# The value product of the forgetting-attention heads in float32r: value parts side by side, softmax weights split at PSUM eviction

## The chip, the cores and the metric

The kernel runs on one core of a Trainium2 chip. The metric is the device time of one execution in microseconds (us), the median of several runs. A core has TensorE for matrix products (PE; PEld is its weight load), VectorE (DVE), ScalarE (ACT) and GpSimd (POOL) for elementwise work, and SyncE (SP), which here issues the DMA transfers. TensorE reads its operands from the on-chip memory SBUF and writes to PSUM; GpSimd doesn't read PSUM in this kernel. The engines run on their own and wait for each other by semaphores.

## The reference

Two layers of a decoder trunk, 256 tokens of width 1024, all in float32. A layer is a half-step SwiGLU feed-forward part, a mixer and a second feed-forward part. The mixer projects the normalized input once (`W_in`), splits the result into three groups of attention heads (A: 4 heads, B: 4, C: 8, head width 64) and projects their outputs back (`W_out`). The change concerns group C, forgetting attention:

```python
def forgetting_attention(q, k, v, log_f):
    c = jnp.cumsum(log_f, axis=1).transpose(0, 2, 1)
    def block(i):
        ...
        s = jnp.einsum('bqhd,bkhd->bhqk', qb, k).astype(jnp.float32) * scale
        s = s + cq[..., None] - c[:, :, None, :]
        s = jnp.where((key_pos[None, :] <= qpos[:, None])[None, None], s, -jnp.inf)
        p = jax.nn.softmax(s, axis=-1).astype(v.dtype)
        return jnp.einsum('bhqk,bkhd->bqhd', p, v)
    ...
# in the mixer:
    o_c = forgetting_attention(cq, ck, cv.reshape(B, S, C_HEADS, HEAD_DIM), log_f)
    o_c = o_c * jax.nn.sigmoid(cg)
    return jnp.concatenate([o_a, o_b, o_c], axis=-1) @ w_out
```

## The kernel before

**Numbers.** The large products are done in float32r, a float32 format with a shortened mantissa. A float32 operand x is written as a high part (x converted to float32r) and a low part (x minus the high part, converted as well), and a product is the sum of three: high by high, high by low, low by high (`mm3`, L295). Weights arrive as `raw` tiles; ScalarE makes the high part `wh` (L117), VectorE the low part `wl` (L121), some units ahead of their use (`pump`). Scores, transposes and value products of the heads are plain float32 matmuls. `mm(o, l, r)` (L292) computes l transposed times r: l is loaded as weights, r streams through, and every matmul of this kind has L293 in the profile.

**Order.** The order of the instructions on each engine is written out by hand, one queue per engine, each worked off in order. In the mixer the eight projection chunks `iq, ib, b, a, ck, cq, cv, cg` follow one another; each takes two PSUM banks of the tag `gu` (4 banks in rotation) and 4 steps, and a `post_` function then moves the result out. `post_cv` (L819) moves the values of the C heads with ScalarE into `va`, whose slots 5 to 12 are the C heads' (slot 0 is A's, 1 to 4 are B's), each 64 columns and a column of ones, with which the value product also gives the sum of the softmax weights. The A and B heads run as side work between steps of the projection, on PSUM banks of the tag `acc`.

**The C heads** run after the projection, from L966, on the banks of `gu`, with the output projection of A's and B's results between them as filler: `out_halves` yields after every 12 matmuls into the `acc` banks, and after every second half it splits one more unit of weights (`W.pump`). In turn i of the loop (L970 to L985) come:

- `scores(i)`: two matmuls into a bank; VectorE adds the mask and takes the maximum (L848);
- `flip(i-1)`: TensorE transposes the three 128x128 blocks of the softmax weights p (L862), and one copy takes them to SBUF as `pT` (L864): on ScalarE for odd heads, on VectorE for even ones;
- `exps(i)`: two exponentials on ScalarE (L855, L856);
- the next 12 matmuls of the output projection;
- `values(i-1)`: three matmuls, pT's blocks as weights against 65 columns of `va`; VectorE takes the reciprocal of the sums (L878) and, for each half of the tokens, multiplies by it and by the gate `sg` on the way out of PSUM (L884);
- from time to time `outT` (transposes of a finished pair of heads, L895, and its split into high and low, L902 and L903) and `c_T` (the transposes of later heads' queries and keys, L962, L963).

After the loop, `tail` finishes the output projection.

Of the kernel before, what the change touches and what calls it, by code (L numbers as in the profile page):

```python
# [10 lines left out]
F32 = mybir.dt.float32  # L11
F32R = mybir.dt.float32r
I32 = mybir.dt.int32
AF = mybir.ActivationFunctionType
ALU = mybir.AluOpType
# [3 lines left out]
P = 128  # L19
# [122 lines left out]
def kernel(ctx: ExitStack, tc: tile.TileContext, x, ffn1_norm, ffn1_w_gate, ffn1_w_up, ffn1_w_down,  # L142
# [3 lines left out]
    cp = ctx.enter_context(tc.tile_pool(name="cp", bufs=1))  # L146
# [6 lines left out]
    at = ctx.enter_context(tc.tile_pool(name="at", bufs=1))  # L153
    pp = ctx.enter_context(tc.tile_pool(name="pp", bufs=2))
# [3 lines left out]
    V, A, G, T = nc.vector, nc.scalar, nc.gpsimd, nc.tensor  # L158

    def bank(tag):  # L160
        return psum.tile([P, 512], F32, name="ps_" + tag, tag=tag)

    def tmp(n):
        return tp.tile([P, 512], F32, name="tmp", tag="tmp")[:, :n]
# [14 lines left out]

    ones = cp.tile([P, P], F32, name="ones")  # L180
    G.memset(ones, 1.0)
    minus_half = cp.tile([P, 32], F32, name="minus_half")
    G.memset(minus_half, -0.5)
    nc.scalar.dma_start(cst[:, 0:P], const[:, 0:P])
# [96 lines left out]
    causal = cp.tile([P, 3 * P], F32, name="causal")  # L281
    cqa = [at.tile([P, 8, 66], F32, name=f"cqa{t}", tag=f"cqa{t}") for t in range(2)]
    cka = [at.tile([P, 8, 66], F32, name=f"cka{t}", tag=f"cka{t}") for t in range(2)]
    va = [at.tile([P, 13, 65], F32, name=f"va{t}", tag=f"va{t}") for t in range(2)]
    for t in range(2):
        G.memset(cqa[t][:, :, 65:66], 1.0)
        G.memset(cka[t][:, :, 64:65], 1.0)
        G.memset(va[t][:, :, 64:65], 1.0)

    hres = xp.tile([P, KT, S], F32, name="hres")  # L290

    def mm(o, l, r, start, stop):  # L292
        T.matmul(o, l, r, start=start, stop=stop, skip_group_check=True)  # L293
# [253 lines left out]
    def mixer(l, norm, nxt):  # L547
# [12 lines left out]
        def heads(ap, n):  # L560
            return ap.rearrange("p (h d) -> p h d", h=n)
# [28 lines left out]
        def evac(dst, ps, t, scale=None):  # L590
            A.activation(dst, ps, AF.Copy, scale=norm.r[:, t:t + 1])
# [226 lines left out]

        def post_cv(ps):  # L819
            for t in range(2):  # L820
                evac(va[t][:, 5:13, 0:64], heads(ps[t], 8), t)

        def post_cg(ps):
            hr = sm.tile([P, 2], F32, name="hr", tag="hr")
# [9 lines left out]
        def run_heads(hs, qk, tag, emit=None, lag=1):  # L834
            pj, pt, op = {}, {}, {}

            def scores(i):

                kind, h = hs[i]
                q, k = qk(h)  # L840
                b = bank(tag)
                mm(b[:, 0:P], q[:, 0:P], k[:, 0:P], True, True)
                mm(b[:, P:3 * P], q[:, P:S], k[:, 0:S], False, True)
                mask = st["amask"] if kind == "A" else causal
                s = tmp(3 * P)
                nm = sm.tile([P, 2], F32, name="nm", tag="nm")
                for t, c in enumerate((slice(0, P), slice(P, 3 * P))):
                    V.tensor_tensor_reduce(s[:, c], b[:, c], mask[:, c], -1.0, 3e38, op0=ALU.add, op1=ALU.min,  # L848
                                           accum_out=nm[:, t:t + 1])
                pj[i] = (s, nm)  # L850

            def exps(i):
                s, nm = pj[i]
                p = pp.tile([P, 3 * P], F32, name="p", tag="p", bufs=2)
                A.activation(p[:, 0:P], s[:, 0:P], AF.Exp, bias=nm[:, 0:1], scale=-1.0)  # L855
                A.activation(p[:, P:3 * P], s[:, P:3 * P], AF.Exp, bias=nm[:, 1:2], scale=-1.0)  # L856
                pj[i] = p

            def flip(i):
                b = bank(tag)  # L860
                for j in range(3):
                    T.transpose(b[:, j * P:(j + 1) * P], pj[i][:, j * P:(j + 1) * P], ident)  # L862
                d = pp.tile([P, 3 * P], F32, name="pT", tag="pT")
                (A.copy if i % 2 == (emit is None) else V.tensor_copy)(d, b[:, :3 * P])  # L864
                pt[i] = d
                del pj[i]

            def values(i):
                kind, h = hs[i]
                vi = dict(A=0, B=1 + h, C=5 + h)[kind]  # L870
                e = i % 2
                b = bank(tag)[:, :130].rearrange("p (t c) -> p t c", t=2)
                d = pt.pop(i)
                mm(b[:, 0], d[:, 0:P], va[0][:, vi], True, True)
                mm(b[:, 1], d[:, P:2 * P], va[0][:, vi], False, False)
                mm(b[:, 1], d[:, 2 * P:3 * P], va[1][:, vi], False, True)
                ri = sm.tile([P, 2], F32, name="ri", tag="ri")
                V.reciprocal(ri, b[:, :, 64])  # L878
                if e == 0:
                    op[i // 2] = pp.tile([P, 2, P], F32, name="o", tag="o")  # L880
                o = op[i // 2][:, :, e * HD:(e + 1) * HD]
                if kind == "C":
                    for t in range(2):
                        V.scalar_tensor_tensor(o[:, t], b[:, t, 0:64], ri[:, t:t + 1],  # L884
                                               st["sg"][:, t, h * HD:(h + 1) * HD], op0=ALU.mult, op1=ALU.mult)
                else:
                    V.tensor_tensor(o, b[:, :, 0:64], ri[:, :, None].to_broadcast([P, 2, HD]), op=ALU.mult)

            def outT(i):
                kind, h = hs[2 * i]  # L890
                k = dict(A=0, B=2, C=4)[kind] + h // 2
                o = op.pop(i)
                b = bank(tag)
                for t in range(2):
                    T.transpose(b[:, t * P:(t + 1) * P], o[:, t], ident)  # L895
                if k < 6:
                    hh = hp.tile([P, S], F32R, name="oh", tag="hh")
                    hl = hp.tile([P, S], F32R, name="ol", tag="hl")
                else:
                    both = tp.tile([P, 512], F32R, name="ohl", tag="tmp")  # L900
                    hh, hl = both[:, :S], both[:, S:]
                A.copy(hh, b[:, :S])  # L902
                V.tensor_tensor(hl, b[:, :S], hh.bitcast(F32), op=ALU.subtract)  # L903
                oT[k] = (hh, hl)

            if emit is None:
                return scores, exps, flip, values, outT
            for i, (kind, h) in enumerate(hs):
                emit(i, lambda i=i: (scores(i), exps(i)))
                emit(i + lag, lambda i=i: flip(i))  # L910
                emit(i + lag + 1, lambda i=i: values(i))
                if i % 2:
                    emit(i + lag + 3, lambda i=i: outT(i // 2))

        oT = {}
        posts = dict(iq=post_iq, ib=post_ib, a=post_a, b=post_b, ck=post_ck, cq=post_cq, cv=post_cv, cg=post_cg)
        for name, cols in CHUNKS:
            n = sum(c[1] for c in cols)
            ps = [bank("gu") for _ in range(2)]
# [71 lines left out]
    def before_mixer(l):  # L991
        if l == 0:
            turn_gains(1)
            turn_gains(2)
            V.memset(causal[:, P:2 * P], 0.0)
            for t in range(2):
                V.tensor_scalar(causal[:, 2 * t * P:(2 * t + 1) * P], future, NEG, None, op0=ALU.mult)
        mixer_tables(l)
# [4 lines left out]
    norm = Norm(0, 0)  # L1003
# [35 lines left out]
    for mp in range(4):  # L1039
        ks = range(2 * mp, 2 * mp + 2)  # L1040
# [30 lines left out]
    for l in range(DEPTH):  # L1071
        norm = ffn(norm, lambda: Norm(1, l), lambda: before_mixer(l), g0 if l == 0 else None)
        norm = mixer(l, norm, lambda: Norm(2, l))
        norm = ffn(norm, (lambda: Norm(0, l + 1)) if l + 1 < DEPTH else None)
# [35 lines left out]
```

## Time and profile before

| | |
|---|---|
| median of 3 runs | 1068.8 us (1068.74 to 1068.98) |
| the profiled execution | 1069.04 us, of which the profile's span is 1067.3 us |
| PE busy | 1059.1 us |
| DVE, ACT busy | 820.6 us, 583.6 us |

How to read it: the profile is of one execution. Busy time is the time in which an engine has an instruction under way; TensorE's matmuls overlap, so the length of one record is not what it costs in a row of them, and the step from one start to the next is. The granted clock is 1.00 at full speed. In a row of a group, the last column before the bar is the count, then come the busy time in us, the mean length in ns, and the idle time of the engine just before.

### The profile page before, as it was taken

What the parts mean: (1) busy time and instruction counts of PE and PEld (TensorE: products, weight loads), DVE (VectorE), ACT (ScalarE), POOL (GpSimd) and SP (SyncE); (2) the same over time, 40 slices, a digit from 0 to 9 for tenths busy, and PEclk for the clock granted to TensorE, in tenths of its full rate; (3) what the DMA queues carried; (4) which work ended last, traced back from release to release, by engine and by line L of the source; (5) the groups of instructions that cost most, each with busy time, mean ns of one, the idle gap of its engine ahead of it and who ended that gap; (6) DMA issues with size and microseconds to landing.
All of it is one profiled execution on the core that took longest, in us unless ns stands there. A gap on an engine that the chain in (4) does not pass through costs nothing.

```text
span 1067.3 us, 16804 instructions
## 1 busy us (share of the span) xinstructions
PE 1059.1 (99%) x6571; PEld 944.9 (89%) x6571; DVE 820.6 (77%) x1547; ACT 583.6 (55%) x998; POOL 162.0 (15%) x188
## 2 busy tenths in 40 slices
PE   9999999999999999999999999999999999999998
PEld 8999999987889899999989999999877998888887
DVE  5998777779766797777779877777796668977774
ACT  5665554666554565555456555546765455655551
POOL 2004000277400100000010200003865000000000
PEclk9999999999999999999999999999999999999999
DMA  9576464464332365554645565555554313664631
GB/s 323 203 238 205 157 233 151 148 211 157 121 117 80 119 223 178 191 198 158 198 158 184 190 226 167 189 173 176 164 170 141 119 41 121 235 235 150 207 119 39
DMA packets 130911, 181.79 MB, mean 170 GB/s; under 512 B 7008, under 2 KB 104720, under 8 KB 130832
## 3 DMA queue, kind: packets, MB, share of 16 engines
q1 hardware_dynamic: 130512, 180.65, 50.1%
q8 instruction: 51, 0.84, 0.3%
q14 instruction: 28, 0.23, 0.1%
q10 hardware_dynamic: 320, 0.08, 0.0%
HBM read 179.67 MB, written 1.05 MB: 169 GB/s over the span
## 4 chain that ended last, share of the span: by engine, by line
PE 97%; DVE 1%; DMA 1%; ACT 0%; SPq 0%; issue 0%
PE ps_gu L293 64%; PE ps_acc L293 31%; PE ps_gu L962 1%; DVE xhl L320 1%; DMA xin<-in_x_dram 1%; PE ps_acc L862 0%; PE ps_gu L862 0%; PE ps_acc L598 0%; DVE hres L352 0%; ACT xhl L317 0%; PE ps_gu L895 0%; PE ps_acc L383 0%; PE ps_acc L895 0%; DVE tmp L424 0%; ACT rb L349 0%
## 5 line engine op out<-in xcount | busy, mean ns | idle before, releaser
L121 DVE TENSOR_TENSOR wl<-raw,wh 128x1024 fp32r<-128x1024 f32 (+2 forms) x343 | 418.4, 1227 | 20.6 <-ACT wh L117 20.3
L293 PE MATMUL ps_gu<-xhl,wh 128*128 128x512 f32 (+1 forms) x1408 | 352.7, 392 | 3.5 <-DVE tmp L424 2.6
L117 ACT CAST wh<-raw 128x1024 fp32r<-128x1024 f32 (+2 forms) x343 | 345.1, 1034 | 12.3 <-PE ps_gu L293 6.8
L293 PEld LDWEIGHTS ps_gu<-xhl,wh 128*128 128x128 f32 x1408 | 253.6, 189 | 51.6 <-DVE xhl L320 2.9
L293 PEld LDWEIGHTS ps_gu<-xhl,wl 128*128 128x128 f32 x1400 | 191.5, 190 | 13.5
L293 PE MATMUL ps_gu<-xhl,wl 128*128 128x256 f32 x1400 | 197.3, 283 | 0.0
L293 PE MATMUL ps_gu<-wh,xhl 128*128 128x512 f32 (+2 forms) x512 | 163.7, 385 | 0.0
L424 DVE TENSOR_TENSOR tmp<-ps_gu,tmp 128x256 f32<-128x256 f32 x175 | 74.1, 424 | 111.2 <-ACT tmp L423 110.9
L293 PE MATMUL ps_acc<-hl,wh 128*128 128x256 f32 x528 | 149.7, 284 | 0.0
L293 PE MATMUL ps_acc<-hh,wh 128*128 128x256 f32 x528 | 149.4, 283 | 0.0
L293 PE MATMUL ps_acc<-hh,wl 128*128 128x256 f32 x528 | 149.4, 283 | 0.0
L423 ACT COPY tmp<-ps_gu 128x256 f32<-128x256 f32 x175 | 64.7, 370 | 128.6 <-PE ps_gu L293 123.1
L293 PEld LDWEIGHTS ps_gu<-wh,xhl 128*128 128x128 f32 x512 | 94.8, 188 | 22.1 <-issue 7.3
L293 PEld LDWEIGHTS ps_acc<-hl,wh 128*128 128x128 f32 x528 | 101.4, 192 | 0.3
L293 PEld LDWEIGHTS ps_acc<-hh,wl 128*128 128x128 f32 x528 | 101.4, 192 | 0.0
L293 PEld LDWEIGHTS ps_acc<-hh,wh 128*128 128x128 f32 x528 | 101.4, 192 | 0.0
L293 PE MATMUL ps_gu<-wl,xhl 128*128 128x512 f32 (+2 forms) x256 | 95.8, 374 | 0.0
L331 POOL TENSOR_TENSOR ssacc<-ssacc,tmp 128x512 f32<-128x512 f32 x10 | 12.9, 1294 | 509.8 <-ACT tmp L329 329.8
L431 ACT ACTIVATE tmp<-tmp 128x256 f32<-128x256 f32 x88 | 36.8, 418 | 85.2 <-DVE tmp L429 85.2
L440 ACT CAST hh<-tmp 128x256 fp32r<-128x256 f32 x80 | 32.6, 407 | 87.9 <-DVE tmp L436 87.9
L293 PEld LDWEIGHTS ps_gu<-wl,xhl 128*128 128x128 f32 x256 | 48.3, 189 | 6.3
L429 DVE TENSOR_TENSOR tmp<-tmp,rb 128x256 f32<-128x256 f32 x88 | 37.8, 430 | 3.0
(241 smaller groups left out, 1204.2 us busy)
## 6 DMA issues: line engine op xcount, KB each, us to landing
raw<-in_ffn_w_down_dram SPq DMA_DIRECT2D x44, 1024.0 KB, 6.7
raw<-in_ffn_w_gate_dram SPq DMA_DIRECT2D x43, 1024.0 KB, 7.0
raw<-in_ffn_w_up_dram SPq DMA_DIRECT2D x43, 1024.0 KB, 5.2
raw<-in_w_in_dram SPq DMA_DIRECT2D x24, 1024.0 KB, 5.2
raw<-in_w_out_dram SPq DMA_DIRECT2D x8, 1024.0 KB, 4.9
raw<-in_w_in_dram SPq DMA_DIRECT2D x4, 768.0 KB, 4.8
raw<-in_w_in_dram SPq DMA_DIRECT2D x4, 656.0 KB, 4.4
xin<-in_x_dram SPq DMA_DIRECT2D x4, 256.0 KB, 5.2
```

The lines of the kernel that those rows point to most:

```text
L117: self.nc.scalar.copy(hv, src)
L121: (engine or self.nc.vector).tensor_tensor(lv, self.srcs[self.n_low], hv.bitcast(F32), op=ALU.subtract)
L293: T.matmul(o, l, r, start=start, stop=stop, skip_group_check=True)
L320: V.scalar_tensor_tensor(self.l[:, m], hres[:, m] if src is None else src, gT[:, self.col + m:self.col + m + 1], self.h[:, m].bitcast(F32) ...
L331: G.tensor_tensor(self.acc, self.acc, sq, op=ALU.add)
L423: A.copy(o, ps[:, 1])
L424: V.tensor_tensor(o, ps[:, 0], o, op=ALU.add)
L429: V.tensor_tensor(t_, t_, norm.rb, op=ALU.mult)
L431: A.activation(th, t_, AF.Tanh, scale=0.5)
L440: (V.tensor_copy if late else A.copy)(hh, t_)
L962: T.transpose(b[:66, i * S + t * P:i * S + (t + 1) * P], src[t][:, 2 * hp_ + i, :], ident)
```

## The change

- The values of the C heads move out of `va` (now 5 slots) into new float32r tiles `vc`, one for each half of the tokens: per head a high part and a low part side by side, each 66 columns: 64 of the value, one that is 1 in the high part and 0 in the low part, and one that is 0. The constant columns are written once at the start (a new memset `zeros` on GpSimd, two copies per tile on VectorE).
- `post_cv`: ScalarE writes the high part, VectorE the low part (PSUM times the norm factor, minus the high part).
- `flip` for C heads: ScalarE copies PSUM to the high half of `pT` (float32r), then VectorE subtracts that from the PSUM block into the low half. For A and B heads it stays as it was.
- `values` for C heads: six float32r matmuls in place of three float32 ones. For each block, the high softmax weights against both value parts (132 columns), then the low weights against the high value part (66 columns). The result has two halves per token block; ScalarE copies the second one (64 columns for each half of the tokens) to SBUF, VectorE adds the first one to it, and the two final multiplications read that sum from SBUF in place of PSUM.

```diff
+    zeros = cp.tile([P, 32], F32, name="zeros")
+    G.memset(zeros, 0.0)
...
-    va = [at.tile([P, 13, 65], F32, name=f"va{t}", tag=f"va{t}") for t in range(2)]
+    va = [at.tile([P, 5, 65], F32, name=f"va{t}", tag=f"va{t}") for t in range(2)]
+    vc = [at.tile([P, 8, 2, 66], F32R, name=f"vc{t}", tag=f"vc{t}") for t in range(2)]
...
+        V.tensor_copy(vc[t][:, :, :, 64:66], zeros[:, 0:32].rearrange("p (a b c) -> p a b c", a=8, b=2))
+        V.tensor_copy(vc[t][:, :, 0, 64], ones[:, 0:8])
...
         def post_cv(ps):
             for t in range(2):
-                evac(va[t][:, 5:13, 0:64], heads(ps[t], 8), t)
+                h, lo = vc[t][:, :, 0, 0:64], vc[t][:, :, 1, 0:64]
+                evac(h, heads(ps[t], 8), t)
+                V.scalar_tensor_tensor(lo, heads(ps[t], 8), norm.r[:, t:t + 1], h.bitcast(F32), op0=ALU.mult,
+                                       op1=ALU.subtract)
...
-                d = pp.tile([P, 3 * P], F32, name="pT", tag="pT")
-                (A.copy if i % 2 == (emit is None) else V.tensor_copy)(d, b[:, :3 * P])
+                if hs[i][0] == "C":
+                    d = pp.tile([P, 2, 3 * P], F32R, name="pTC", tag="pT")
+                    A.copy(d[:, 0], b[:, :3 * P])
+                    V.tensor_tensor(d[:, 1], b[:, :3 * P], d[:, 0].bitcast(F32), op=ALU.subtract)
+                else:
+                    d = pp.tile([P, 2, 3 * P], F32, name="pT", tag="pT")[:, 0]
+                    (V.tensor_copy if i % 2 else A.copy)(d, b[:, :3 * P])
...
-                b = bank(tag)[:, :130].rearrange("p (t c) -> p t c", t=2)
                 d = pt.pop(i)
-                mm(b[:, 0], d[:, 0:P], va[0][:, vi], True, True)
-                mm(b[:, 1], d[:, P:2 * P], va[0][:, vi], False, False)
-                mm(b[:, 1], d[:, 2 * P:3 * P], va[1][:, vi], False, True)
+                if kind == "C":
+                    b = bank(tag)[:, :264].rearrange("p (t c) -> p t c", t=2)
+                    for j in range(3):
+                        t, v, ks = j > 0, vc[j // 2][:, h], slice(j * P, (j + 1) * P)
+                        mm(b[:, int(t)], d[:, 0, ks], v, j == 0, False)
+                        mm(b[:, int(t), 0:66], d[:, 1, ks], v[:, 0], False, j == 2)
+                    low = tmp(P).rearrange("p (t d) -> p t d", t=2)
+                    A.copy(low, b[:, :, 66:130])
...
                 if kind == "C":
+                    V.tensor_tensor(low, b[:, :, 0:64], low, op=ALU.add)
                     for t in range(2):
-                        V.scalar_tensor_tensor(o[:, t], b[:, t, 0:64], ri[:, t:t + 1],
+                        V.scalar_tensor_tensor(o[:, t], low[:, t], ri[:, t:t + 1],
                                                st["sg"][:, t, h * HD:(h + 1) * HD], op0=ALU.mult, op1=ALU.mult)
```

More of the change, by code (lines that the diff above doesn't have):

```diff
@@ L869, in values @@
                 kind, h = hs[i]
-                vi = dict(A=0, B=1 + h, C=5 + h)[kind]
                 e = i % 2
-                b = bank(tag)[:, :130].rearrange("p (t c) -> p t c", t=2)
                 d = pt.pop(i)
-                mm(b[:, 0], d[:, 0:P], va[0][:, vi], True, True)
-                mm(b[:, 1], d[:, P:2 * P], va[0][:, vi], False, False)
-                mm(b[:, 1], d[:, 2 * P:3 * P], va[1][:, vi], False, True)
+                if kind == "C":
[6 more added lines that the diff above has]
+                    A.copy(low, b[:, :, 66:130])
+                else:
+                    vi = dict(A=0, B=1 + h)[kind]
+                    b = bank(tag)[:, :130].rearrange("p (t c) -> p t c", t=2)
+                    mm(b[:, 0], d[:, 0:P], va[0][:, vi], True, True)
+                    mm(b[:, 1], d[:, P:2 * P], va[0][:, vi], False, False)
+                    mm(b[:, 1], d[:, 2 * P:3 * P], va[1][:, vi], False, True)
                 ri = sm.tile([P, 2], F32, name="ri", tag="ri")
```

## The prediction

> **What bounds the kernel now.** I read the page first: span, busy shares, granted clock, chain.
>
> ```profile
> span 1067.3 us, 16804 instructions
> PE 1059.1 (99%) x6571; PEld 944.9 (89%) x6571; DVE 820.6 (77%) x1547; ACT 583.6 (55%) x998; POOL 162.0 (15%) x188
> ...
> PEclk9999999999999999999999999999999999999999
> ...
> PE 97%; DVE 1%; DMA 1%; ACT 0%; SPq 0%; issue 0%
> ```
>
> TensorE sets the end: 97% of the chain is its own work, at full clock. So every nanosecond that the change adds to or takes from the TensorE stream counts, and work of VectorE and ScalarE counts only where TensorE comes to wait for it. VectorE, at 77%, is the one that could get there. Next, the busy times of the two stretches in which the C heads run, one per layer (columns: stretch, length, then busy time and instructions of PE, PEld, DVE, ACT, POOL, the clock, DMA):
>
> ```profile
> 312.00:344.00 32.00, 32.00 (x269) 31.29 (x268) 21.07 (x71) 15.83 (x32) 0.00 (x0) 1.00 0.21 67
> 840.00:872.00 32.00, 32.00 (x269) 31.30 (x268) 21.34 (x72) 15.86 (x32) 0.00 (x0) 1.00 0.20 68
> ```
>
> No gap in TensorE in either. Then the timeline of one head period of layer 0, TensorE alone (start, length, instruction, count of records; lengths overlap, so I use differences of starts):
>
> ```profile
> 323.92 0.82 PE L293 MATMUL ps_gu<-cT 66*128 66x128 f32 x4
> 324.58 0.49 PE L862 MATMUL ps_gu<-cst,p 128*128 128x128 f32 x3
> ...
> 325.03 0.28 PE L293 MATMUL ps_acc<-ol,wh 128*128 128x256 f32 x1
> ...
> 326.23 0.28 PE L293 MATMUL ps_acc<-oh,wl 128*128 128x256 f32 x1
> 326.35 0.78 PE L293 MATMUL ps_gu<-va,pT 128*128 128x65 f32 x6
> 326.96 0.60 PE L962 MATMUL ps_gu<-cst,cqa 128*66 128x128 f32 x4
> ```
>
> The three float32 value matmuls leave six records, so each is two passes, and they hold TensorE for 326.96 - 326.35 = 0.61 us: 0.102 us a pass. The 128x256 float32r matmuls step by (326.23 - 325.03) / 10 = 0.120 us. This group of six is what the change replaces.
>
> **The change part by part.** *TensorE.* Per C head six records of float32 go (3 x two passes, 65 columns), and six float32r matmuls come: three of 132 columns (high weights times both value parts), three of 66 (low weights times the high value part). Sixteen heads in all (8 in each of 2 layers). What one costs depends on whether streaming or the weight load limits it. Streaming, from float32r with 512 columns:
>
> ```profile
> 199.62 0.62 PE L293 MATMUL ps_gu<-wh,xhl 128*128 128x512 f32 x2
> 200.07 0.39 PE L293 MATMUL ps_gu<-wl,xhl 128*128 128x512 f32 x1
> 200.30 0.62 PE L293 MATMUL ps_gu<-wh,xhl 128*128 128x512 f32 x2
> ```
>
> Three take 200.30 - 199.62 = 0.68, 0.227 each. With 0.120 at 256 columns that is a line of 0.107 / 256 = 0.42 ns a column and 0.013 us fixed: 132 columns would stream in 0.068 us, 66 in 0.041. Loads:
>
> ```profile
> L293 PEld LDWEIGHTS ps_gu<-va,pT 128*128 128x128 f32 x96 | 12.1, 191 | 0.0
> L293 PEld LDWEIGHTS ps_acc<-oh,wh 128*128 128x128 f32 x96 | 18.3, 190 | 0.0
> ...
> 863.65 0.19 PEld L293 LDWEIGHTS ps_acc<-oh,wh 128*128 128x128 f32 x1
> 863.75 0.19 PEld L293 LDWEIGHTS ps_acc<-ol,wh 128*128 128x128 f32 x1
> ```
>
> A load of 128 columns lasts 191 ns in a float32 pass and 190 in float32r, and two float32r loads with nothing to hold them back start 0.10 apart. So I take the old passes to be limited by the load already (0.102 although 65 columns are few), and the new ones by the same load. The number of loads stays six. Lowest, 0.102 each: nothing gained or lost. Highest on this reading, the 0.120 of 256 columns: 6 x 0.120 = 0.72, +0.11 a head. I take 0.105, next to the load rows: 0.63, +0.02 a head, **+0.3 us** over 16 heads (0 to +1.8). The Trainium skill, "TensorE: Matmul & The Clock Gate", section "LDWEIGHTS (loading the stationary operand)", puts a load at its columns over 1.2 GHz, 0.107 us for 128; the trace's 0.102 a pass is a little below that, and by the page the term would be 16 x (6 x 0.107 - 0.61) = +0.5 us.
>
> *The softmax weights on their way to those matmuls.* Before, one copy (ScalarE for odd heads, VectorE for even ones); after, a copy on ScalarE, then a subtraction on VectorE that needs it, in series. They must fit under the 12 output-projection matmuls that run between the transposes and the value matmuls.
>
> ```profile
> 325.17 0.48 ACT L864 COPY pT<-ps_gu 128x384 f32<-128x384 f32 x1 [0.67 <-PE ps_gu L862]
> ...
> 325.49 0.08 DVE L848 DVE_READ_ACCUMULATOR2_ANT nm<- 128x1 f32 x1
> 325.49 1.22 DVE L121 TENSOR_TENSOR wl<-raw,wh 128x1024 fp32r<-128x1024 f32 x1
> 327.16 0.17 DVE L878 RECIPROCAL ri<-ps_gu 128x2 f32<-128x2 f32 x1 [0.45 <-PE ps_gu L293]
> 327.37 0.48 DVE L884 SCALAR_TENSOR_TENSOR o<-ps_gu,ri,sg 128x64 f32<-128x64 f32 x2
> 328.04 0.69 DVE L963 COPY cT<-ps_gu 66x512 f32<-66x512 f32 x1 [0.19 <-PE ps_gu L962]
> ...
> L864 DVE COPY pT<-ps_gu 128x384 f32<-128x384 f32 x8 | 4.4, 553 | 0.0
> L903 DVE TENSOR_TENSOR ol<-ps_gu,oh 128x256 fp32r<-128x256 f32 x4 | 1.7, 425 | 0.1
> L887 DVE TENSOR_TENSOR o<-ps_acc,ri 128x128 f32<-128x128 f32 x16 | 4.7, 291 | 0.6
> ...
> 861.98 0.75 PEld L293 LDWEIGHTS ps_gu<-va,pT 128*128 128x128 f32 x6
> 862.10 0.78 PE L293 MATMUL ps_gu<-va,pT 128*128 128x65 f32 x6
> ```
>
> The copy ends at 325.17 + 0.48 = 325.65. The subtraction stands in VectorE's queue behind the score reductions (ended 325.57) and ahead of the weight split wl. Its price is that of a copy of 384 columns, 0.56 (256 columns cost 0.425): 325.69 to 326.25. A load starts 0.12 ahead of its matmul, and only the second matmul of the group needs the low part, so its load is due about 0.10 after the first one's at 326.23: at 326.33. **Slack about 0.1 us**, if VectorE's queue is on time. Whatever is late at that point holds the value matmuls, and behind them everything on TensorE.
>
> *The way out.* After the matmuls ScalarE copies the low half (128x128 out of PSUM), VectorE adds it (0.29, the L887 row), and the two final multiplies read SBUF instead of PSUM. ScalarE's copy stands behind its weight cast in every second head:
>
> ```profile
> 324.12 0.37 ACT L902 CAST oh<-ps_gu 128x256 fp32r<-128x256 f32 x1 [1.40 <-PE ps_gu L895]
> ...
> 326.25 1.03 ACT L117 CAST wh<-raw 128x1024 fp32r<-128x1024 f32 x1
> ```
>
> so it runs 327.28 to about 327.6 (at most the 0.37 of 256 columns); the add waits behind the reciprocal until then, and o is done near 328.4 instead of 327.85. Queued behind on VectorE are the cT copy, the next reductions and the next subtraction: all some 0.4 late in such a head, and with 0.1 of slack the next value matmuls wait. VectorE's idle time gives part of it back:
>
> ```profile
> 324.58:328.49 3.91, 3.91 (x34) 3.81 (x33) 3.22 (x11) 2.70 (x5) 0.00 (x0) 1.00 0.00 0
> 328.49:331.74 3.25, 3.25 (x28) 3.15 (x27) 1.96 (x9) 1.18 (x3) 0.00 (x0) 1.00 0.00 0
> ```
>
> Of these two periods (7.16 us) VectorE is busy 5.18; it gets two subtractions and two adds (1.7) and loses one copy (0.55): 6.3, still below 7.16, so it doesn't become the bound; only its order in time hurts. Stall per head: lowest 0; highest, in heads with a cast the wait for ScalarE's copy and the add in full, 0.37 + 0.29 less the slack of 0.1, 0.56, and 0.1 in the others: mean 0.33, or 5.3 us over 16. Since the late work falls in every second head and mostly into idle time, I take 0.05 a head, **+0.8 us**.
>
> *Elsewhere.* The values' own split adds two VectorE operations of 128x512 out of PSUM a layer, some 0.8 each (twice 256 columns). They fall in the last projection chunk, where VectorE waits like this:
>
> ```profile
> 297.92 0.17 DVE L878 RECIPROCAL ri<-ps_acc 128x2 f32<-128x2 f32 x1 [1.78 <-PE ps_acc L293]
> ...
> 301.64 0.17 DVE L878 RECIPROCAL ri<-ps_acc 128x2 f32<-128x2 f32 x1 [2.09 <-PE ps_acc L293]
> ```
>
> 3.9 us idle for 1.6 of work: nothing; without that cover they would delay the A heads' copies by up to 1.6 a layer. The PSUM banks that they hold longer aren't asked for until cT, a whole chunk later. The new memset and four constant copies run at the start:
>
> ```profile
> 0.87 0.12 POOL L183 MEMSET minus_half<- 128x32 f32 x1
> ...
> 4.34 0.72 PEld L1012 LDWEIGHTS ps_acc<-cst,xin 128*128 128x128 f32 x4 [0.29 <-DMA cst<-in_const_dram]
> ```
>
> The memset is as long as minus_half's, 0.12 (0.06 to the next one's start), and TensorE's first real work waits for a DMA until 4.34: nothing. No DMA is added or moved. Heads A and B keep their instructions.
>
> Sum: 1067.3 + 0.3 + 0.8 = 1068.4 of span. The profiled execution took 1069.04, 1.74 more than its span and 0.24 above the median of the runs, so its time would be 1070.1 and the median **1069.9 us**.
>
> **The rivals.** *Narrow float32r isn't one pass (slower).* No float32r matmul of this kernel has fewer than 256 columns, so nothing shows that the rate holds at 132 and 66. Its place is the 16 value groups. If such a matmul runs at float32's rate, the price is read from the scores at 323.92: 128 and 256 columns in 0.66 us, 1.72 ns a column. Then 132 columns take 0.227 and 66 take 0.113, three of each 1.02, +0.41 a head, +6.6 us; longer periods leave the stall term at about 0.2: 1068.8 + 6.8 = **1075.6**. It decides as soon as the streaming of a narrow matmul costs more than the load, that is from twice the rate on (132 x 0.84 = 0.11 us). For it: the case is unmeasured. Against it: cost has followed columns on one line down to 256, and a float32 pass of few columns is as cheap as its load.
>
> *VectorE's queue order holds the value matmuls (slower).* The upper end of the stall term, 5.3 + 0.3: **1074.4**. For it: slack of 0.1 us against 0.4 of lateness; against it: over 0.8 us of idle VectorE in every two heads, which soaks it up.
>
> *Loads hide and streaming decides (faster).* Six matmuls at 3 x (0.068 + 0.041) = 0.33 instead of 0.61: -0.28 a head, -4.5, with the stall +0.8: **1065.1**. Against it stand the load rows, 0.10 apart. The Trainium skill, same page, section "Weight-path perf modes — Fast Weight Load (FWL) and DoubleRow", gives quick loads to 128 weights of any type but FP32 and no gain for four-byte elements; the equal 190 and 191 ns agree, and were float32r let in, this would be the rival that comes true.
>
> **How the numbers follow.** Forecast 0.53, narrow rate 0.23, queue order 0.14, hidden loads 0.08; 0.02 for anything else. A change below 0.2% (2.1 us) can't be told from none here. The forecast is +1.1 with 0 to +1.8 for the passes and 0 to about 2 for the stall: nearly all of it within 0.2% (0.46), a little above (0.06), 0.01 below. The slower rivals add 0.35 and 0.01 for the rest, the faster one 0.08: faster 0.09, same 0.49, slower 0.42. The forecast's own range is 1068.3 to 1071.5. To leave out no more than 2 in 10 the range must reach the slow rivals: 1068.0 to 1076.0 holds the forecast, the queue order and most of the narrow rate, and leaves out the faster case.
>
> **What would show it.** In the new profile the value group of six should still span about 0.63 us from its first start to the next one's; 1.0 means the narrow rate, 0.33 hidden loads. Idle time of PE or PEld ahead of the value matmuls, put down to the pTC subtraction, is the stall: some 0.8 us in all, 5 if queue order wins. VectorE should be busy some 25.7 us in the first stretch instead of 21.07 (8 x (0.56 + 0.29) more, four copies of 0.55 less). The forecast is wrong if the time leaves 1068.3 to 1071.5, or if it stays inside with a group far from 0.63 and stalls making up for it.

## The result and the profile after

Median 1070.46 us over 20 runs (1070.09 to 1071.02), before 1068.95 over 20 runs (1068.60 to 1069.24): ratio 1.0014, 95% interval 1.0008 to 1.002. That is 1.5 us more. The forecast was 1.1 us more, 1069.9, with a range of 1068.0 to 1076.0. The profiled execution took 1070.09, the quickest of its 20. The page after:

```profile
span 1068.3 us, 16859 instructions
PE 1060.2 (99%) x6571; PEld 945.9 (89%) x6571; DVE 829.7 (78%) x1579; ACT 591.0 (55%) x1022; POOL 161.7 (15%) x189
...
PEclk9999999999999999999999999999999999999999
...
PE 96%; DVE 1%; DMA 1%; ACT 1%; issue 0%; ACTq 0%; DVEq 0%
```

TensorE still sets the end, with as many records as before (6571): six passes per head went and six matmuls came. VectorE has 9 us more work, ScalarE 7. In the changed kernel the matmuls are at L298, `flip`'s ScalarE copy at L873, its subtraction at L874, ScalarE's copy of the second half at L892, the reciprocal, the add and the final multiplies at L900, L905 and L907. TensorE's timeline of layer 0, each value group with the instruction that follows it (start, length, instruction, records):

```profile
316.27 0.76 PE L298 MATMUL ps_gu<-vc,pTC 128*128 128x132 f32 x6
316.87 0.90 PE L298 MATMUL ps_gu<-cT 66*128 66x128 f32 x4
319.36 0.76 PE L298 MATMUL ps_gu<-vc,pTC 128*128 128x132 f32 x6
319.95 0.63 PE L985 MATMUL ps_gu<-cst,cqa 128*66 128x128 f32 x4
...
326.56 0.83 PE L298 MATMUL ps_gu<-vc,pTC 128*128 128x132 f32 x6
327.23 0.63 PE L985 MATMUL ps_gu<-cst,cqa 128*66 128x128 f32 x4
...
339.65 0.94 PE L298 MATMUL ps_gu<-vc,pTC 128*128 128x132 f32 x6
340.43 0.36 PE L298 MATMUL ps_acc<-oh,wh 128*128 128x256 f32 x1
```

Half of the groups hold TensorE for about 0.59 us (319.95 - 319.36), less than the 0.61 of the float32 passes. The one at 326.56 takes 0.67, the last of the layer 0.78; two more take 0.68 and 0.62. In all, the eight groups of a layer take 0.39 us more than eight times 0.59 in layer 0 and 0.38 in layer 1. No idle time stands at these rows: a wait inside a chain of overlapping matmuls shows as a longer step from start to start only. VectorE and ScalarE in the same stretch as in the prediction:

```profile
324.07 0.27 ACT L892 COPY tmp<-ps_gu 128x128 f32<-128x128 f32 x1 [0.80 <-PE ps_gu L298]
...
324.37 0.17 DVE L900 RECIPROCAL ri<-ps_gu 128x2 f32<-128x2 f32 x1 [1.20 <-ACT tmp L892]
324.45 0.27 DVE L905 TENSOR_TENSOR tmp<-ps_gu,tmp 128x128 f32<-128x128 f32 x1
324.76 0.48 DVE L907 SCALAR_TENSOR_TENSOR o<-tmp,ri,sg 128x64 f32<-128x64 f32 x2
325.16 0.42 DVE L926 TENSOR_TENSOR ol<-ps_gu,oh 128x256 fp32r<-128x256 f32 x1
...
326.04 0.55 DVE L874 TENSOR_TENSOR pTC<-ps_gu,pTC 128x384 fp32r<-128x384 f32 x1
```

Even the reciprocal waits for ScalarE's copy. So VectorE's queue is late: the subtraction, for which 325.69 was reckoned, starts at 326.04. Of these 0.35 us, 0.21 is the later place of the whole head (its group starts at 326.56, before at 326.35); 0.14 is lateness against TensorE. It ends at 326.59, where the load that needs it is due at 326.56 - 0.12 + 0.10 = 326.54. That is the group of 0.67.

There is a second difference, at the start: the matmuls that sum the first feed-forward part's squares, before and after:

```profile
17.91 0.58 PE L293 MATMUL ps_acc<-ones,ssacc 128*128 128x1 f32 x4
```

```profile
18.20 0.58 PE L298 MATMUL ps_acc<-ones,ssacc 128*128 128x1 f32 x4 [0.31 <-DVE ssacc L1083]
```

Call the time from the first transposes of queries after the projection (L962 before, L985 after) to the last transposes of outputs (L895, L918) the C stage. Its two ends in layer 0, before and after:

```profile
308.42 0.60 PE L962 MATMUL ps_gu<-cst,cqa 128*66 128x128 f32 x4
...
341.29 0.38 PE L895 MATMUL ps_gu<-cst,o 128*128 128x128 f32 x2
```

```profile
308.59 0.60 PE L985 MATMUL ps_gu<-cst,cqa 128*66 128x128 f32 x4
...
341.94 0.38 PE L918 MATMUL ps_gu<-cst,o 128*128 128x128 f32 x2
```

It takes 341.29 - 308.42 = 32.87 us before and 341.94 - 308.59 = 33.35 after; in layer 1, 32.91 and 33.35. The two stages make 0.92 of the span's 1.0 us; the rest arises in the first 20 us, and 0.17 of it is left where the first stage begins. From the norm sums to the C stage it takes 308.42 - 17.91 = 290.51 before and 308.59 - 18.20 = 290.39 after, so the split of the values in `post_cv` costs TensorE nothing, as forecast.

### The profile page after: what moved, and what is told of

It reads as the page before. It is cut to its first block, busy times and chain, and to the rows that moved or that the text cites. A ratio compares the mean times of both kernels' runs of the same rounds, so it can differ in the third digit from the quotient of the medians.

```text
span 1068.3 us, 16859 instructions
## 1 busy us (share of the span) xinstructions
PE 1060.2 (99%) x6571; PEld 945.9 (89%) x6571; DVE 829.7 (78%) x1579; ACT 591.0 (55%) x1022; POOL 161.7 (15%) x189
## 4 chain that ended last, share of the span: by engine, by line
PE 96%; DVE 1%; DMA 1%; ACT 1%; issue 0%; ACTq 0%; DVEq 0%
PE ps_gu L298 63%; PE ps_acc L298 31%; DMA raw<-in_ffn_w_gate_dram 1%; PE ps_gu L985 1%; DVE xhl L325 1%; PE ps_acc L870 0%; PE ps_gu L870 0%; PE ps_acc L603 0%; DVE hres L357 0%; DMA tmp<-in_ffn_norm_dram 0%; ACT xhl L322 0%; DVE tmp L1083 0%; PE ps_gu L918 0%; PE ps_acc L918 0%; PE ps_acc L388 0%
## 5 line engine op out<-in xcount | busy, mean ns | idle before, releaser
L298 PE MATMUL ps_gu<-xhl,wh 128*128 128x512 f32 (+1 forms) x1408 | 352.8, 392 | 3.5 <-DVE tmp L429 2.6
L298 PEld LDWEIGHTS ps_gu<-xhl,wh 128*128 128x128 f32 x1408 | 253.6, 189 | 51.6 <-DVE xhl L325 2.9
L298 PEld LDWEIGHTS ps_gu<-xhl,wl 128*128 128x128 f32 x1400 | 191.5, 190 | 13.5
L298 PE MATMUL ps_gu<-xhl,wl 128*128 128x256 f32 x1400 | 197.3, 283 | 0.0
L298 PE MATMUL ps_gu<-wh,xhl 128*128 128x512 f32 (+2 forms) x512 | 163.7, 385 | 0.0
L298 PE MATMUL ps_acc<-hl,wh 128*128 128x256 f32 x528 | 149.7, 284 | 0.0
L298 PE MATMUL ps_acc<-hh,wl 128*128 128x256 f32 x528 | 149.4, 283 | 0.0
L298 PE MATMUL ps_acc<-hh,wh 128*128 128x256 f32 x528 | 149.4, 283 | 0.0
L298 PEld LDWEIGHTS ps_gu<-wh,xhl 128*128 128x128 f32 x512 | 94.8, 188 | 22.0 <-issue 7.3
L298 PEld LDWEIGHTS ps_acc<-hl,wh 128*128 128x128 f32 x528 | 101.3, 192 | 0.3
L298 PEld LDWEIGHTS ps_acc<-hh,wl 128*128 128x128 f32 x528 | 101.4, 192 | 0.0
L298 PEld LDWEIGHTS ps_acc<-hh,wh 128*128 128x128 f32 x528 | 101.3, 192 | 0.0
L298 PE MATMUL ps_gu<-wl,xhl 128*128 128x512 f32 (+2 forms) x256 | 95.7, 374 | 0.0
L298 PEld LDWEIGHTS ps_gu<-wl,xhl 128*128 128x128 f32 x256 | 48.3, 189 | 6.4
L441 DVE TENSOR_TENSOR tmp<-tmp 128x256 f32<-128x256 f32 x88 | 37.6, 427 | 3.0
```

Of the source, the lines that this page charges most:

```text
L441: V.tensor_tensor(t_, summed(u), t_, op=ALU.mult)
```

## The experiments

Theory: the value groups cost what they did, being limited by weight loads, and the loss is the wait for the late subtraction. First rival: narrow float32r matmuls are dearer in themselves. Second rival, after the result: something at the start. There were twelve runs; the kernel before ran beside them, with medians of 1068.89 to 1068.96. A time is the median, with the lowest and the highest in brackets.

### The same kernel again

> The changed kernel once more, unaltered, for a second profile. In the first one the C stage of each layer is 0.47 us longer than before and another 0.2 us lies in the first 20 us of the span; the profiled execution was the quickest of its 20. Theory: the C stages again give 0.47 each, the start varies from execution to execution. Rival: the start is longer by 0.2 us or more in this execution too. Time 1070.5, ratio to before 1.0014.

1070.48 (1070.10 to 1071.13). The C stages again take 33.35 and 33.33, and the norm sums come at 18.20 again. The lateness at the start is not one execution's accident.

### High weights first

```diff
-    for j in range(3):
-        t, v, ks = j > 0, vc[j // 2][:, h], slice(j * P, (j + 1) * P)
-        mm(b[:, int(t)], d[:, 0, ks], v, j == 0, False)
-        mm(b[:, int(t), 0:66], d[:, 1, ks], v[:, 0], False, j == 2)
+    for k in range(2):
+        for j in range(3):
+            t, v, ks = int(j > 0), vc[j // 2][:, h], slice(j * P, (j + 1) * P)
+            mm(b[:, t, 0:66] if k else b[:, t], d[:, k, ks], v[:, 0] if k else v, j + k == 0, j + k == 3)
```

> The six matmuls of a value group in another order: the three with the high softmax weights first, then the three with the low ones. Same work, but the low half is due two matmuls (0.2 us) later. Theory (the value group waits for the VectorE subtraction in some heads; 0.08 us in three or four heads and 0.2 in the last of a layer): the groups take 0.59 us in all heads but the last, and the time falls by 0.6 to 0.8, to 1069.7. Rival (narrow float32r matmuls cost more than the float32 passes in themselves, and the order doesn't matter): 1070.5.

1069.52 (1069.39 to 1069.99): every run is below every run of the unaltered kernel beside it. Its timeline, the two groups that had waited:

```profile
326.79 0.76 PE L298 MATMUL ps_gu<-vc,pTC 128*128 128x132 f32 x6
327.38 0.63 PE L986 MATMUL ps_gu<-cst,cqa 128*66 128x128 f32 x4
...
339.70 0.76 PE L298 MATMUL ps_gu<-vc,pTC 128*128 128x132 f32 x6
340.29 0.36 PE L298 MATMUL ps_acc<-oh,wh 128*128 128x256 f32 x1
```

0.59 in both, and in all sixteen heads 0.58 to 0.60, the last of a layer too, where a wait was still expected. The C stages fall to 32.99 each, by 0.36. The wait for the low half is real and is worth 0.72 us in the profile by the C stages, 0.76 by the groups. The median fell by 0.96, more than the 0.6 to 0.8 expected; the part above 0.76 lies outside the groups, and nothing shows where.

### Without the way out

```diff
-    low = tmp(P).rearrange("p (t d) -> p t d", t=2)
-    A.copy(low, b[:, :, 66:130])
...
-    V.tensor_tensor(low, b[:, :, 0:64], low, op=ALU.add)
-    V.scalar_tensor_tensor(o[:, t], low[:, t], ri[:, t:t + 1],
+    V.scalar_tensor_tensor(o[:, t], b[:, t, 0:64], ri[:, t:t + 1],
```

> ScalarE's copy of the second half and VectorE's add are left out, and the final multiplies read PSUM as before; the product of high weights with low values is computed but not added. The subtraction in flip stays. Theory (the subtraction is late because VectorE's queue is pushed back by the way out): groups of 0.59 in all heads, no wait of 0.2 in the last head of a layer, time 1069.7. Rival (the subtraction is late by the serial copy and subtraction alone): the waits stay, 1070.5.

1069.88 (1069.54 to 1070.53). Fifteen of sixteen groups take 0.58 to 0.59, one in layer 0 still 0.69: there VectorE's `ol` subtraction waited 0.42 for ScalarE ahead of it. The reciprocal no longer waits for ScalarE either. So copy and subtraction in series just fit; they come late because of what is queued ahead of the subtraction, mostly the way out.

### Constants later

The zeros memset stands after GpSimd's other memsets here, and the four constant copies in the middle of the first feed-forward part.

> The zeros memset goes behind GpSimd's other memsets and the four constant copies of VectorE into the middle of the first feed-forward part. Theory (the constants at the start cost nothing; the differences there are the DMA's): no change, 1070.5. Rival (they push the start by 0.2 to 0.4 us): 1070.1 to 1070.3.

1070.50 (1070.32 to 1070.68), and the norm sums come at 18.72. The place of these instructions is not what makes the start late.

### The kernel before, twice more

> The kernel before, unaltered, for a second profile. All five profiles with the new value product reach the norm sums of the first feed-forward part (the matmuls of ones with ssacc) at 18.2 to 18.7 us, the one of before at 17.9. Theory (the DMA's start varies from execution to execution): a value between 17.9 and 18.7 here. Rival (the change makes the start later): 17.9 again.

> The kernel before a third time, for the same question: by the theory between 17.9 and 18.7, by the rival 17.9.

1068.73 and 1069.22, one execution each. The norm sums come at 17.64 and 17.77, neither of them between 17.9 and 18.7: with the first profile 17.6 to 17.9, never 18.2. The start does vary, but by less than the difference: the change makes it later.

### 66 columns in all six

```diff
-    mm(b[:, int(t)], d[:, 0, ks], v, j == 0, False)
+    mm(b[:, int(t), 0:66], d[:, 0, ks], v[:, 0], j == 0, False)
```

> As e2_no_way_out, and the high weights meet only the high value part: 66 columns stream in place of 132 in three of the six matmuls; the product of high weights with low values is not computed. Theory (the weight load limits a group): groups stay 0.59 us, time as e2_no_way_out within 0.2. Rival (streaming counts): at 0.42 ns a column 66 x 3 x 16 columns are 1.3 us, at the float32 rate of 1.72 ns a column 5.4 us; groups of 0.51 or 0.25.

The edit stands on top of that of the run without the way out. 1069.90 (1069.54 to 1070.11), against 1069.88 with 132. Its groups in layer 0, for example:

```profile
327.17 0.76 PE L298 MATMUL ps_gu<-vc,pTC 128*128 128x66 f32 x6
327.76 0.63 PE L982 MATMUL ps_gu<-cst,cqa 128*66 128x128 f32 x4
```

0.59 again. Columns are free here: at 132 and at 66 columns streaming does not set the price of a float32r matmul, and its rate is nothing like float32's.

### Three matmuls a group

The matmuls with the low softmax weights are left out.

> The three matmuls with the low softmax weights are left out of each group (their product isn't computed); split, copies and the way out stay. Theory (each matmul costs its weight load of 0.098 us, and the wait for the low half goes): groups of 0.29 to 0.30 us, time 1070.5 - 0.8 - 16 x 0.29 = 1065.0. Rival (the 132-column matmuls cost twice the 66-column ones or more): groups of 0.39 or more, 1066.6 or more.

1065.01 over five runs (1064.62 to 1066.07), ratio 0.9963 (0.995 to 0.9977), the number that was expected. The profiled execution was the slowest of them.

```profile
320.51 0.45 PE L298 MATMUL ps_gu<-vc,pTC 128*128 128x132 f32 x3
320.80 0.60 PE L984 MATMUL ps_gu<-cst,cqa 128*66 128x128 f32 x4
```

0.29 for three: 0.097 for each, wide or narrow. So the group's price is its number of matmuls, whatever their columns. Each matmul has a weight load of its own, and such loads start 0.10 apart when nothing holds them back, as the prediction's rows show, so the load is the likely limit; no run here tells it from another fixed price of a matmul.

### The weight buffers 128 bytes further on

What was left at the start besides the instructions is the layout. The tile `zeros` (128 bytes a partition) is allocated ahead of the raw weight tiles, which so begin at byte 8064 of SBUF in place of 7936: a multiple of 128 and no longer of 256. Everything allocated behind them moves as well. The kernel before with an unused tile in that place:

```diff
+    cp.tile([P, 32], F32, name="pad")
     ones = cp.tile([P, P], F32, name="ones")
```

> The kernel before with one unused tile of 128 bytes ahead of the raw tiles in SBUF, which shifts them by 128 bytes, as the new zeros tile does; no instruction differs. In three profiles of the kernel before the norm sums of the first feed-forward part start at 17.6 to 17.9 us, in six with the new value product at 18.2 to 19.6, and SyncE's issues of whole weight tiles in the first 15 us last 1.67 and 1.45 before, 1.97 and 1.74 after. Theory (the shifted destination makes the weight DMAs slower): issues of 1.97 and 1.74, norm sums at 18.2 or later, time 1069.3 to 1069.5. Rival (another part of the change does it): 17.6 to 17.9, 1068.95.

1069.74 (1069.51 to 1070.27), the kernel before beside it 1068.90 (1068.48 to 1069.34): all runs above all runs, +0.84 us with not one instruction changed. It is above the expected 1069.3 to 1069.5. SyncE's issues of two whole weight tiles, in the kernel before, then in this one (start, length of the issue):

```profile
9.09 1.67 SPq L91 DMA_DIRECT2D raw<-in_ffn_w_gate_dram  x1
10.81 1.45 SPq L91 DMA_DIRECT2D raw<-in_ffn_w_up_dram  x1
```

```profile
8.85 1.97 SPq L91 DMA_DIRECT2D raw<-in_ffn_w_gate_dram  x1
10.86 1.74 SPq L91 DMA_DIRECT2D raw<-in_ffn_w_up_dram  x1
```

The two issues ahead of these vary from execution to execution in either layout (1.4 to 2.5 us), so the transfers themselves are the better sign. The stretch from 8 to 14 us, before and here (last column: GB/s moved by the DMA):

```profile
8.00:14.00 6.00, 5.87 (x42) 5.33 (x41) 4.52 (x8) 5.59 (x11) 1.28 (x1) 1.00 1.13 352
```

```profile
8.00:14.00 6.00, 5.72 (x40) 5.24 (x40) 4.05 (x8) 4.94 (x10) 1.28 (x1) 1.00 1.18 298
```

In the six profiles with the raw tiles at a multiple of 256 this rate is 352 to 358, in the eight with the shift 298 to 303. And what waits for such a tile, ScalarE's split of the next weights, before and here; after it come VectorE's wl, the sum of squares, and then:

```profile
12.23 1.06 ACT L117 CAST wh<-raw 128x1024 fp32r<-128x1024 f32 x1 [0.31 <-DMA raw<-in_ffn_w_gate_dram]
```

```profile
12.72 1.05 ACT L117 CAST wh<-raw 128x1024 fp32r<-128x1024 f32 x1 [0.76 <-DMA raw<-in_ffn_w_gate_dram]
...
18.39 0.58 PE L294 MATMUL ps_acc<-ones,ssacc 128*128 128x1 f32 x4 [0.65 <-DVE ssacc L1061]
```

The same 1.97 and 1.74 stand in the changed kernel. Almost only the start feels it: later the weights come in ahead of their use. The C stages here take 32.86 and 32.90, as before, and the second begins 528.63 us after the first, before 528.55.

### The zeros tile moved, and both cures

```diff
-    zeros = cp.tile([P, 32], F32, name="zeros")
+    zeros = at.tile([P, 32], F32, name="zeros", tag="zeros")
```

> The changed kernel with the zeros tile behind the raw tiles in SBUF, so that these lie where they lay before. Theory (shifted destination): norm sums at 17.6 to 17.9, time 1070.0, 0.4 to 0.5 less than the changed kernel. Rival: 18.2 or later, 1070.5.

1069.52 (1069.34 to 1069.92), 0.9 less than the changed kernel, about twice what was expected; the two issues last 1.67 and 1.45 again, and the rate from 8 to 14 us is 356. The norm sums came at 18.08, a little above the expected range, in a profiled execution that was the slowest of its 11.

> Both cures together: high weights first in each value group, and the zeros tile behind the raw tiles. Theory: 1069.52 of e1_high_first less 0.4 to 0.5: 1069.05, at most 0.2 above the kernel before, which is what the C stages still cost (0.1 each). Rival: 1069.5.

1068.87 (1068.50 to 1069.14), ratio 1.0 (0.9991 to 1.0008); every run is below every run of the one with the zeros tile moved alone. The C stages take 33.01 and 33.00.

> As e10_hf_moved, with 256 unused bytes ahead of the raw tiles, so that they start at a multiple of 512 bytes (8192) in place of 256 (7936). If the start's DMAs gain from it as they lost by the shift to 128, the time is 1068.6 to 1068.9; if 256 is enough for them, 1069.05.

1068.77 (1068.62 to 1069.28), ratio 0.9999 (0.999 to 1.0008). The number lies where a gain was expected, but that of the kernel without the 256 bytes, 1068.87, lies there too, and the issues last 1.67 and 1.45 as with 256: no gain that can be told. Without the three matmuls the product is incomplete, so among the complete versions none clearly beats the kernel before.

## Why the prediction was right, and where it wasn't

- **The price of the groups.** That columns don't limit a group was right and is shown by the 66-column and three-matmul runs; they fit "limited by the load already". The term was forecast at +0.3 (0.105 a matmul); a matmul took 0.098, under the float32 pass's 0.102, and all of that and a little more is given back: the float32 instructions after a group step 0.02 to 0.06 wider. The widest such step, before and after:

```profile
323.70 0.39 PE L895 MATMUL ps_gu<-cst,o 128*128 128x128 f32 x2
323.92 0.82 PE L293 MATMUL ps_gu<-cT 66*128 66x128 f32 x4
```

```profile
323.86 0.44 PE L918 MATMUL ps_gu<-cst,o 128*128 128x128 f32 x2
324.14 0.82 PE L298 MATMUL ps_gu<-cT 66*128 66x128 f32 x4
```

It is 0.22 before and 0.28 after. With the waits gone the C stages are 0.12 and 0.08 longer than before: **+0.2**, near the forecast, but by the step after the group, which wasn't foreseen, and not by dearer matmuls. Why this step is wider is open. The rivals of the narrow rate and of hidden loads are out: groups of 0.59, neither 1.0 nor 0.33.
- **The stall.** Forecast +0.8, measured 0.39 + 0.38 = **+0.77**, and in the place named: the low half's load, from VectorE's queue order. Two details differ. The reciprocal, too, waits for ScalarE's copy, which wasn't foreseen; and the largest single wait, 0.19, is in the last head of a layer, where `ol`'s subtraction stands ahead, and not in every second head alike. The queue-order rival named the same mechanism with too high a price: idle VectorE time did soak up most of it. That the size fits so well is luck: the 0.05 us a head was picked between 0 and 0.33 and not worked out from the rows.
- **The step that failed** is in "Elsewhere", which put the start at nothing: "The memset is as long as minus_half's, 0.12 ... nothing. No DMA is added or moved." The memset and the copies cost nothing that can be told, as the run with them moved showed. What the new tile did to the addresses behind it wasn't considered: it moved the destination of every weight DMA, and that cost **0.6 to 0.9 us**. It is +0.84 in the kernel before with the padding alone. Moving the tile brought the changed kernel from 1.52 to 0.62 above the kernel before beside it, and the one with the high weights first from 0.56 above to 0.03 below.
- **The sum.** 0.2 + 0.8 + 0.8 is 1.8 against 1.5 measured; the two cures together take off 1070.46 - 1068.87 = 1.6. Single terms are known to no better than some 0.3 us, as the 0.9 and 0.6 for the same shift show. The forecast of 1.1 more was inside its own range because its two terms came out about right and the layout that it left out cost less than 1 us; it was 0.4 low. The change is within 0.2%, as held likeliest. That so small a change "can't be told from none" was too careful: here 0.84 us separated all runs of one kernel from all of the other.
- **What would show it.** VectorE's busy time in the first stretch was forecast to rise to 25.7 us; the same window after:

```profile
312.00:344.00 32.00, 32.00 (x266) 31.14 (x265) 24.05 (x84) 19.48 (x44) 0.00 (x0) 1.00 0.17 53
```

24.05, so 3.0 more in place of 4.6: the lengths of the instructions that start in this window add up to 3.6 us more only, and more of their ends overlap. The stall was to appear as idle time of PE or PEld, which was wrong: it appears only as a longer step.

## What to carry to other kernels

A float32 product whose streamed side is narrow may already cost its number of passes, two for each matmul and each with its weight load, and not its columns. Two float32r matmuls per block in its place then save nothing, and the splitting and adding are extra work. So count loads before columns. Within an accumulation group, put the matmuls whose operands come last at the end: here that alone took the wait away. And a new tile, however small, shifts every buffer allocated behind it; before explaining a difference by instructions, compare addresses, or run the old kernel with padding.

## What the runs showed of the hardware that wasn't expected

- A shift of the weight buffers from a multiple of 256 to one of 128 bytes slowed their transfers at the start: 298 to 303 GB/s between 8 and 14 us in place of 352 to 358. By the trace's packet records, the median packet of 512 bytes, which carry most of what moves in this time, took 31 to 32 ns in place of 27, and one of 1024 bytes, between 14 and 25 us, 51 in place of 46. After 30 us it is 46 in both. The issue of a 1 MB weight DMA took 1.97 us in place of 1.67 and 1.74 in place of 1.45; later in the kernel such an issue takes 0.37, so at the start it probably waits for the packets ahead of it, and its 18 and 20% more are those of the 512-byte packets. The Trainium skill, "DMA: Bandwidth & Descriptors", section "How a descriptor splits into AXI transactions", tells of bus transactions of 256 bytes that must start at multiples of 256, so that a descriptor that starts elsewhere begins with bytes that aren't used and still cost beats of 32 bytes; it speaks of reads. If writes are cut alike, a row of 1024 bytes takes 36 beats in place of 32 by that page, an estimate of 12% more; its packets grew by 11%. That this is the mechanism was not tried; that the shift alone does it was.
- A float32r matmul with weights of 128 columns took 0.097 to 0.098 us with 66 and with 132 streamed columns, where 256 took 0.120.
- A matmul that waits inside a row of overlapping matmuls left no idle time in the profile: groups of 0.67 and 0.78 us stood beside groups of 0.59 without any, and the order of the six matmuls alone took the difference away.
